# Trading the order of the two matmul widths between neighbouring output chunks of a decoder trunk on one core

## The chip, the cores and the metric

The kernel runs on one core of one Trainium2 chip. The metric is the device time of one execution in microseconds; less is better. Three executions of the kernel before took 2847.95, 2847.97 and 2849.41 us, median 2847.97.

## What is computed

A decoder trunk of two layers over 256 tokens of width 2048, in float32, with 256 memory tokens to attend to. Nearly all of the work is matrix products with weights that are read once:

```python
for l in range(DEPTH):                       # DEPTH = 2, D_MODEL = 2048, D_FF = 8192
    hn = rms_norm(x, mix_norm_g[l])
    x = x + (even_mixer(hn, ...) if l % 2 == 0 else odd_mixer(hn, ...))
    x = x + cross_attention(rms_norm(x, xattn_norm_g[l]), mem_n, xq_w[l], xk_w[l], xv_w[l], xo_w[l])
    x = x + sq_relu_mlp(rms_norm(x, mlp_norm_g[l]), mlp_w1[l], mlp_w2[l])
return rms_norm(x, final_norm_g)
```

`even_mixer` is a gated convolution beside a differential attention, `odd_mixer` a gated short convolution; both end in a product with an output weight (`even_out`, `odd_out`).

## The kernel before

**The product.** Activations lie transposed: 128 partitions of a channel chunk, 256 tokens along the row. A weight column block of 128 outputs is an "output chunk" and needs 16 products over the 16 chunks of the input width (2048 = 16 x 128). To keep float32 accuracy every operand is split in two parts of a shorter format: `hi`, a rounded copy, and `lo`, the rest. TensorE computes hi x hi and hi x lo of the activations in one instruction, because the activation's two parts lie side by side (`act.both(k)`, 512 columns); the weight's rest needs a second one, lo x hi (`act.hi(k)`, 256 columns). So an output chunk is 16 products of 512 columns with weights `whi` and 16 of 256 columns with weights `wlo`, all summed in one PSUM bank; a 256-column product touches the first half of the bank only. Each product has a weight load of its own (PEld in the profile).

**The weights' way.** A chunk's weights come in two halves (g = 0 and 1) of 128 x 1024, enough for eight products each. SyncE's queue loads a half to a `raw` buffer (4 buffers), ScalarE casts it to `whi` (3 buffers, `wspl`), VectorE subtracts to get `wlo` (4 buffers). With three `whi` buffers and two halves a chunk, the first half of chunk c+1 goes where the second half of chunk c-1 was, and the second half of chunk c+1 goes where the first half of chunk c was. ScalarE and VectorE work through their instructions in order.

**Long runs.** `long_run` (L219) writes a chunk's 32 products: 15 of 512 columns (L229), 16 of 256 (L231), and the sixteenth of 512 as the last (L233). `proj_long` (L236) uses it in the mixers' and the cross-attention's output projections and in `odd_in`, `Chunk.run` (L968) in the MLP and at the end of `odd_mixer`.

**Pieces.** `proj_group` and `proj` (L206, L241) take the two halves one after the other, so that a chunk can begin when its first half is there. `wide_piece` (L193) writes a half: eight products of 512 and eight of 256; in the last half the eighth of 512 comes last. `cross` uses it for the 32 query chunks `xq` (16 a layer).

**The MLP.** `mlp` (L1139) goes through four quarters of 2048 hidden channels in each of the two layers. A quarter begins with 16 first-product chunks (`firsts`, L1235, c = 0 to 15), and here the order on every engine is that of the code. While TensorE runs chunk c, the other engines do this in order:

- ScalarE copies half of the PSUM bank of chunk c-1 (`sum`), casts the first half of chunk c+1 (`n.hi(0)`), casts its second half (`n.hi(1)`), and squares the output of chunk c-1 (`uu`).
- VectorE adds and scales the output of chunk c-1 (two instructions on `sum`), then makes `n.lo(0)` and `n.lo(1)` of chunk c+1.
- For c = 5, 9 and 13, behind that, VectorE does two additions on `uu` (L1278, L1279), ScalarE casts the result to `hs` (L1280) and VectorE subtracts (L1281).

The second half of a quarter (steps of a Strassen form, and chunks by `outs[k].run`) calls `long_run` too, without the change's new argument.

Of the kernel before, what the change touches and what calls it, by code (L numbers as in the profile page):

```python
# [10 lines left out]
F32 = mybir.dt.float32  # L11
# [6 lines left out]
P = 128  # L18
D = 2048
S = 256  # L20
# [25 lines left out]
def trunk(ctx: ExitStack, tc: tile.TileContext, d):  # L46
# [38 lines left out]
    ps_mm = ctx.enter_context(tc.tile_pool(name="ps_mm", bufs=4, space=bass.MemoryType.PSUM))  # L85
# [59 lines left out]
    def ordered(i, token):  # L145

        tc.stamp_issue_order_token(i.ins, token)
# [20 lines left out]
    def mm(*a, **k):  # L168
        i = T.matmul(*a, **k)  # L169
        if strict[0]:  # L170
            ordered(i, "pe")
# [18 lines left out]
            ordered(V.tensor_tensor(lo[:, o], raw[:, o], f(hi[:, o]), op=ALU.subtract), "lo")  # L190
        return hi, lo

    def wide_piece(ps, hi, lo, act, k, first, last, between=None):  # L193


        w = [slice(j * P, (j + 1) * P) for j in range(8)]
        for j in range(7 if last else 8):
            mm(ps, hi[:, w[j]], act.both(k + j), start=first and j == 0, stop=False)
        for j in range(8):
            mm(ps[:, :S], lo[:, w[j]], act.hi(k + j), start=False, stop=False)  # L200
        if between:
            between()
        if last:
            mm(ps, hi[:, w[7]], act.both(k + 7), start=False, stop=True)

    def proj_group(srcs, act, order=(0, 1), between=None):  # L206


        pp = [ps_mm.tile([P, 512], F32, tag="mm", name="mm") for _ in srcs]
        for g in order:  # L210
            if g == order[-1] and len(srcs) > 1:
                run_stages(END)
            for src, ps in zip(srcs, pp):
                hi, lo = weights(src[:, g * 1024:(g + 1) * 1024])
                first, last = g == order[0], g == order[-1]
                wide_piece(ps, hi, lo, act, g * 8, first, last, between if last and ps is pp[-1] else None)
        return pp

    def long_run(ps, h, l, act, narrow=False):  # L219

        w = [slice(j * P, (j + 1) * P) for j in range(8)]
        if narrow:
            for k in range(16):
                for part in (act.lo, act.hi):
                    mm(ps[:, :S], h[k // 8][:, w[k % 8]], part(k), start=k == 0 and part == act.lo, stop=False)
            for k in range(16):
                mm(ps[:, :S], l[k // 8][:, w[k % 8]], act.hi(k), start=False, stop=k == 15)
            return ps
        for k in range(15):  # L229
            mm(ps, h[k // 8][:, w[k % 8]], act.both(k), start=k == 0, stop=False)  # L230
        for k in range(16):  # L231
            mm(ps[:, :S], l[k // 8][:, w[k % 8]], act.hi(k), start=False, stop=False)
        mm(ps, h[1][:, w[7]], act.both(15), start=False, stop=True)  # L233
        return ps

    def proj_long(src, act):  # L236
        ps = ps_mm.tile([P, 512], F32, tag="mm", name="mm")
        h, l = zip(*[weights(src[:, g * 1024:(g + 1) * 1024]) for g in range(2)])
        return long_run(ps, h, l, act)

    def proj(src, act):  # L241
        return proj_group([src], act)[0]

    def summed(ps, out=None):

        t = tmp32("sum")
        A.copy(t, ps[:, S:])
        out = t if out is None else out
        V.tensor_tensor(out, ps[:, :S], t, op=ALU.add)
        return out  # L250
# [46 lines left out]
    def joined(*acts):  # L297
        a = Act(0, "")
        a.t = [t for b in acts for t in b.t]
        return a  # L300
# [112 lines left out]
    def even_mixer():  # L413
        xa, ss = Act(NC, "xn"), SumSq()
        w = d["even_in"]
# [224 lines left out]
        cat_a, cat_o = ln["cat"], rr["co"]  # L640
        nxt, nss = Act(NC, "xn"), SumSq()
        cat = joined(cat_a, cat_o)
        for c, ps in enumerate(proj_group([d["even_out"][c] for c in range(3)], cat, (1, 0))):
            residual(c, ps, nxt, nss, "xat0")
        for c in range(3, NC):
# [4 lines left out]
    def odd_mixer(xa, ss):  # L650
        w = d["odd_in"]
        y, m = Act(NC, "y"), Act(NC, "mem")
        begun = [NC, 2 * NC, 0, NC + 1]
        rows = []

        def mean():
# [14 lines left out]
        for c in range(NC):  # L671
# [7 lines left out]
            i = c * 3  # L679
            V.tensor_scalar(uu, cc, col("conv_c_w", i + 2), None, op0=ALU.mult)  # L680
            for j in range(2):
                s = 2 - j
# [26 lines left out]
            V.tensor_tensor(t[:, :, 1], q, f(t[:, :, 0]), op=ALU.subtract)  # L709

        LAST = 4
        for c in range(NC - LAST):
            residual(c, proj_long(d["odd_out"][c], y), None, nss, "xat1")
            if c < 8:
                forms(c)
# [47 lines left out]
        for k in range(NC):  # L763
            last = k + 1 == NC
# [20 lines left out]
            s = st[k + 1]  # L785
# [70 lines left out]
    def cross(l, xa, ss, kmem):  # L856
        keys, vals = kmem
        r = None
        scale = 512 ** -0.5
        oa = joined()  # L860

        def scores(h, q, k):
            v = split(vals[h // 2][:, h % 2], [2, 512])
            pr = []
            for t in range(2):
                tq = slice(t * P, (t + 1) * P)
                ps = ps_at.tile([P, 512], F32, tag="at", name="sx")[:, :S]
                for i in range(4):
                    mm(ps, q[:, 0, i, tq], k[:, 0, i], start=i == 0, stop=False)
                    mm(ps, q[:, 1, i, tq], k[:, 0, i], start=False, stop=False)  # L870
                    mm(ps, q[:, 0, i, tq], k[:, 1, i], start=False, stop=i == 3)
                p, inv = softmax_rows(ps, mem_r["bc"], S, scale)
                V.tensor_scalar(p, p, inv, None, op0=ALU.mult)
                pr.append(p)
            stage(X1, lambda: turn(h, pr, v))

        def turn(h, pr, v):
            pt = ps_at.tile([P, 512], F32, tag="at", name="ptx")
            for t in range(2):
                for kt in range(2):  # L880
                    transpose(out=pt[:, kt * S + t * P:kt * S + (t + 1) * P], in_=pr[t][:, kt * P:(kt + 1) * P],
                              identity=ident)
            pb = pools["att"].tile([P, 2, 512], F32R, tag="pt", name="pb")
            A.copy(pb[:, 0], pt)
            V.tensor_tensor(pb[:, 1], pt, f(pb[:, 0]), op=ALU.subtract)
            stage(X2, lambda: heads_out(h, pb, v))

        def heads_out(h, pb, v):
            if h % 2 == 0:
                oa.t += Act(8, "o").t  # L890
            for i in range(4):
                if i % 2 == 0:
                    bank = ps_at.tile([P, 512], F32, tag="at", name="pox")
                po = bank[:, i % 2 * S:(i % 2 + 1) * S]
                e = slice(i * P, (i + 1) * P)
                for kt in range(2):
                    c = slice(kt * S, (kt + 1) * S)
                    mm(po, v[:, 0, kt, e], pb[:, 0, c], start=kt == 0, stop=False)
                    mm(po, v[:, 1, kt, e], pb[:, 0, c], start=False, stop=False)
                    mm(po, v[:, 0, kt, e], pb[:, 1, c], start=False, stop=kt == 1)  # L900
                if i % 2:
                    oa.put2(4 * h + i - 1, bank)

        for h in range(XH):
            q = half.tile([P, 2, 4, S], F32R, tag="half", name="xq")
            for i in range(4):
                if i == 3:
                    k = split(keys[h // 2][:, h % 2], [4, S])
                s = summed(proj(d[f"xq{l}"][4 * h + i], xa))
                if r is None:  # L910
                    r = rstd(ss.acc, D)
                    strict[0] = True
                V.tensor_tensor(s, s, r, op=ALU.mult)
                A.copy(q[:, 0, i], s)
                V.tensor_tensor(q[:, 1, i], s, f(q[:, 0, i]), op=ALU.subtract)
            stage(X0, lambda h=h, q=q, k=k: scores(h, q, k))
        nxt, nss = Act(NC, "xn"), SumSq()

        for c, ps in enumerate(proj_group([d[f"xo{l}"][c] for c in range(4)], oa)):
            residual(c, ps, nxt, nss, f"mlp{l}")  # L920
        strict[0] = False
        for c in range(4, NC):
            residual(c, proj_long(d[f"xo{l}"][c], oa), nxt, nss, f"mlp{l}")
        return nxt, nss
# [15 lines left out]
    class Chunk:  # L940
# [24 lines left out]
            A.activation(self.l[g], self.raw[g], AF.Copy, scale=-1.0)  # L965
            G.dma_start(out=self.l[g], in_=self.raw[g], accum_op=ALU.add)  # L966

        def run(self, act, pool, tag, narrow=False):  # L968
            self.ps = long_run(pool.tile([P, 512], F32, tag=tag, name="mm"), self.h, self.l, act, narrow)

    class Step:

# [166 lines left out]
    def mlp(l, xa, ss, gname):  # L1139
# [13 lines left out]
        turn = [0]  # L1153
# [69 lines left out]
        for qd in range(4):  # L1223
            seven, closing = qd < ns, qd == 3
            hid, sa, vs = Act(0, "hid"), [], {}
            chunks, outs = firsts[qd], seconds[qd]
# [6 lines left out]
                return vs[c // 4]  # L1233

            for c in range(NC):  # L1235
                chunks[c].run(xa, ps_mm, "mm")
                fetch((Chunk, Step))
                if c in (4, 13) and seven:
                    st[c // 13].load()
# [30 lines left out]
                g = c // 4 - 1  # L1270
# [11 lines left out]
                if seven:  # L1282
                    s = st[0]
# [12 lines left out]
            if seven:  # L1296
# [6 lines left out]
                for k in range(8):  # L1303
                    st[k].run(sevens.pp, hid, sa, k)
                    fetch(Step)
                    w = outs[k]
# [17 lines left out]
                    if k < 7:  # L1324
                        s = st[k + 1]
# [168 lines left out]
```

## Time and profile before

| what | value |
|---|---|
| three executions | 2847.95 to 2849.41 us, median 2847.97 |
| the profiled execution | 2848.45 us, span of its instructions 2846.1 us |
| PE busy | 2834.7 us of the span, 15843 products |
| VectorE (DVE) busy | 2318.1 us, 81% |
| ScalarE (ACT) busy | 1689.5 us, 59% |
| granted TensorE clock | 0.999 |
| DMA | 588 MB, 207 GB/s |

PE is TensorE's products, PEld its weight loads. In a timeline a row's first number is the start in us from the span's start, the second the time to the end of the last of its instructions, and in square brackets stands how long the engine was idle before it and what ended that. A product's own duration in the profile overlaps the next one; what a product costs is the distance from its start to the next one's start. So a row's cost is read from the start of the next row.

### The profile page before, as it was taken

Reading aid. Unit: us, or ns where it says so; the run is one execution under the profiler, and the core shown is the slowest. Engines: PE = TensorE matmul, PEld = TensorE weight load, DVE = VectorE, ACT = ScalarE, POOL = GpSimd, SP = SyncE. Lnnn points to the kernel's source line nnn. Section 1 sums busy time; section 2 is a strip of 40 time slices with the busy share of each in tenths; the row PEclk is TensorE's granted clock in tenths of the full one; section 3 lists DMA queues with packets and bytes.
Section 4 is the critical chain, followed back from the end, with each engine's and each line's share of the span. In section 5 each row is a group of like instructions: output and inputs, shape, how many; then the busy total and the mean of one; then the engine's idle time right before and its main releaser. Section 6 shows DMA issues by size and latency. Waiting matters only on the chain.

```text
span 2846.1 us, 42267 instructions
## 1 busy us (share of the span) xinstructions
PE 2834.7 (100%) x15843; PEld 2478.3 (87%) x15843; DVE 2318.1 (81%) x3602; ACT 1689.5 (59%) x2368; POOL 78.6 (3%) x107
## 2 busy tenths in 40 slices
PE   9999999999999999999999999999999999999998
PEld 8888888898888888888888888888988888888887
DVE  7899987777788888888987787888777888888888
ACT  6665445555565665656654455676556656656566
POOL 0000000000000000000000000000000000000000
PEclk9999999999999999999999999999999999999999
DMA  7455665545686786967765566994456867769676
GB/s 249 160 189 172 192 194 189 171 149 178 195 256 195 223 241 200 266 193 234 214 203 199 196 209 224 253 255 155 150 178 194 253 209 218 234 200 262 199 236 179
DMA packets 213516, 588.23 MB, mean 207 GB/s; under 512 B 18240, under 2 KB 84160, under 8 KB 213312
## 3 DMA queue, kind: packets, MB, share of 16 engines
q1 hardware_dynamic: 200064, 538.54, 58.1%
q0 software_dynamic: 12672, 46.14, 8.2%
q8 instruction: 124, 2.03, 0.3%
q10 hardware_dynamic: 576, 0.85, 0.1%
q14 instruction: 80, 0.66, 0.1%
HBM read 537.23 MB, written 2.10 MB: 189 GB/s over the span
## 4 chain that ended last, share of the span: by engine, by line
PE 97%; DMA 1%; DVE 1%; ACT 1%; issue 0%; SPq 0%; DVEq 0%; POOLq 0%; POOL 0%; ACTq 0%
PE mm L169 77%; PE p L169 13%; PE mmr L169 4%; PE pox L169 1%; PE sx L169 1%; DMA wlo<-raw 0%; PE sc L169 0%; DVE x L59 0%; DMA raw<-w 0%; ACT whi L59 0%; PE nmr L169 0%; PE po L169 0%; DVE wlo L59 0%; DMA raw<-odd_in 0%; DMA x<-xT 0%
## 5 line engine op out<-in xcount | busy, mean ns | idle before, releaser
L59 ACT CAST whi<-raw 128x1024 fp32r<-128x1024 f32 (+1 forms) x849 | 890.6, 1050 | 394.2 <-PE mm L169 297.2
L59 DVE TENSOR_TENSOR wlo<-raw,whi 128x1024 fp32r<-128x1024 f32 (+1 forms) x761 | 924.0, 1220 | 93.2 <-ACT whi L59 82.6
L169 PE MATMUL mm<-xn,whi 128*128 128x512 f32 x3840 | 938.7, 392 | 0.0
L169 PEld LDWEIGHTS mm<-xn,whi 128*128 128x128 f32 x3840 | 702.0, 188 | 133.3 <-DVE xn L59 0.6
L169 PEld LDWEIGHTS mm<-xn,wlo 128*128 128x128 f32 x3840 | 501.1, 191 | 24.0
L169 PE MATMUL mm<-xn,wlo 128*128 128x256 f32 x3840 | 509.1, 283 | 0.0
L59 ACT COPY sum<-mm 128x256 f32<-128x256 f32 x272 | 100.6, 371 | 394.5 <-PE mm L169 394.0
L169 PE MATMUL mm<-hid,whi 128*128 128x512 f32 (+1 forms) x1040 | 253.4, 386 | 0.0
L59 ACT CAST tw<-raws 128x1024 fp32r<-128x1024 f32 x160 | 160.6, 1046 | 145.1 <-DVE raws L59 141.2
L59 DVE TENSOR_TENSOR raws<-raws 128x512 f32<-128x512 f32 x320 | 220.8, 690 | 7.6
L169 PEld LDWEIGHTS mm<-hid,whi 128*128 128x128 f32 x1040 | 193.5, 188 | 36.8
L59 DVE TENSOR_TENSOR sum<-mm,sum 128x256 f32<-128x256 f32 x240 | 100.9, 421 | 146.5 <-ACT sum L59 146.2
L59 DVE TENSOR_TENSOR tw<-raws,tw 128x1024 fp32r<-128x1024 f32 x160 | 189.6, 1222 | 26.2 <-ACT tw L59 24.6
L169 PE MATMUL p<-tw,hs 128*128 128x512 f32 x720 | 189.2, 389 | 0.0
L59 DVE TENSOR_TENSOR x<-x,mm 128x256 f32<-128x256 f32 x255 | 106.9, 420 | 81.7 <-PE mm L169 77.2
L169 PEld LDWEIGHTS p<-tw,hs 128*128 128x128 f32 x720 | 135.2, 188 | 28.0
L966 POOL DMA_DIRECT2D wlo<-raw x88 | 74.9, 855 | 2550.8 <-ACT wlo L59 1847.1
L169 PEld LDWEIGHTS mm<-hid,wlo 128*128 128x128 f32 x1024 | 131.1, 191 | 5.8 <-DMA wlo<-raw 1.1
L169 PE MATMUL mm<-hid,wlo 128*128 128x256 f32 x1024 | 133.1, 283 | 0.4 <-DMA wlo<-raw 0.4
L169 PE MATMUL mm<-mem,whi 128*128 128x512 f32 x512 | 128.5, 393 | 0.0
L169 PE MATMUL mm<-o,whi 128*128 128x512 f32 x512 | 124.7, 392 | 0.0
L59 DVE TENSOR_TENSOR slo<-raws,shi 128x1024 fp32r<-128x1024 f32 x71 | 86.9, 1224 | 38.1 <-ACT shi L59 38.1
(227 smaller groups left out, 3236.6 us busy)
## 6 DMA issues: line engine op xcount, KB each, us to landing
raw<-w SPq DMA_DIRECT2D x384, 512.0 KB, 5.0
raws<-w SPq DMA_DIRECT2D x128, 512.0 KB, 5.2
raw<-odd_in SPq DMA_DIRECT2D x96, 512.0 KB, 4.6
wlo<-raw POOLq DMA_DIRECT2D x88, 512.0 KB, 7.5
raw<-even_in SPq DMA_DIRECT2D x64, 512.0 KB, 4.4
raw<-xk SPq DMA_DIRECT2D x64, 512.0 KB, 4.6
raw<-xq SPq DMA_DIRECT2D x64, 512.0 KB, 4.2
raw<-xo SPq DMA_DIRECT2D x64, 512.0 KB, 3.8
```

What stands on the lines that cost most here:

```text
L59: i = getattr(self.engine, name)(*a, **k)
L169: i = T.matmul(*a, **k)
L966: G.dma_start(out=self.l[g], in_=self.raw[g], accum_op=ALU.add)
```

## The change

`long_run` gets an argument `turn`. With `turn=None` it is as before (15, 16, 1). With `turn=0` all 16 products of 512 columns come first and the 16 of 256 behind them; with `turn=1` one product of 512 comes first, then all 16 of 256, then the other 15 of 512. (The first must be of 512, since it opens the whole bank.) `proj_long` takes the two in turns, starting anew with 0 in each section; the MLP's first products take `c % 2`. Below, a chunk with `turn=0` is called even, one with `turn=1` odd. There are 110 odd ones: 6 in `even_out`, 22 in `odd_in`, 6 in `odd_out`, 6 in `xo` of each layer, and 8 in each of the MLP's eight quarters. The second halves of the query chunks (`fold`) begin with the 256-column products and end with the 512-column ones.

```diff
+        if fold and last:
+            for j in range(8):
+                mm(ps[:, :S], lo[:, w[j]], act.hi(k + j), start=False, stop=False)
+            for j in range(8):
+                mm(ps, hi[:, w[j]], act.both(k + j), start=False, stop=j == 7)
+            return
...
-        for k in range(15):
+        split = 15 if turn is None else 1 if turn else 16
+        for k in range(split):
             mm(ps, h[k // 8][:, w[k % 8]], act.both(k), start=k == 0, stop=False)
         for k in range(16):
-            mm(ps[:, :S], l[k // 8][:, w[k % 8]], act.hi(k), start=False, stop=False)
-        mm(ps, h[1][:, w[7]], act.both(15), start=False, stop=True)
+            mm(ps[:, :S], l[k // 8][:, w[k % 8]], act.hi(k), start=False, stop=split == 16 and k == 15)
+        for k in range(split, 16):
+            mm(ps, h[k // 8][:, w[k % 8]], act.both(k), start=False, stop=k == 15)
         return ps
...
-        return long_run(ps, h, l, act)
+        longs[0] ^= 1
+        return long_run(ps, h, l, act, turn=1 - longs[0])
...
-                s = summed(proj(d[f"xq{l}"][4 * h + i], xa))
+                s = summed(proj(d[f"xq{l}"][4 * h + i], xa, True))
...
-                chunks[c].run(xa, ps_mm, "mm")
+                chunks[c].run(xa, ps_mm, "mm", turn=c % 2)
```

The first place is TensorE in the MLP's second quarter of the first layer, chunk c = 9 of the first products, an odd one. `whi_9745` and `whi_9749` are the two halves' hi parts, `wlo_9751` and `wlo_9753` their lo parts, `xn` the activations. Before:

```order
L169 MATMUL mm_9761<-xn_6711,whi_9745 128x512 x4
L169 MATMUL mm_9761<-xn_6712,whi_9745 128x512 x4
L169 MATMUL mm_9761<-xn_6713,whi_9749 128x512 x4
L169 MATMUL mm_9761<-xn_6714,whi_9749 128x512 x3
L169 MATMUL mm_9761<-xn_6711,wlo_9751 128x256 x4
L169 MATMUL mm_9761<-xn_6712,wlo_9751 128x256 x4
L169 MATMUL mm_9761<-xn_6713,wlo_9753 128x256 x4
L169 MATMUL mm_9761<-xn_6714,wlo_9753 128x256 x4
L169 MATMUL mm_9761<-xn_6714,whi_9749 128x512
```

The same chunk on TensorE now:

```order
L169 MATMUL mm_9761<-xn_6711,whi_9745 128x512
L169 MATMUL mm_9761<-xn_6711,wlo_9751 128x256 x4
L169 MATMUL mm_9761<-xn_6712,wlo_9751 128x256 x4
L169 MATMUL mm_9761<-xn_6713,wlo_9753 128x256 x4
L169 MATMUL mm_9761<-xn_6714,wlo_9753 128x256 x4
L169 MATMUL mm_9761<-xn_6711,whi_9745 128x512 x3
L169 MATMUL mm_9761<-xn_6712,whi_9745 128x512 x4
L169 MATMUL mm_9761<-xn_6713,whi_9749 128x512 x4
L169 MATMUL mm_9761<-xn_6714,whi_9749 128x512 x4
```

Both lo parts are read 14 products earlier in the chunk than before, and the last read of the first half's hi part (`whi_9745`) comes behind all 16 of the 256-column products.

The second place is VectorE at the same time: what it does while TensorE runs chunks 9 and 10. `wlo_9807` and `wlo_9809` belong to chunk 10, `hs` is the combined hidden piece, `mm_9761` the output of chunk 9, `wlo_9862` and `wlo_9864` belong to chunk 11. These rows are the same in both kernels:

```order
L59 TENSOR_TENSOR wlo_9807<-raw_9739,whi_9801 128x1024
L59 TENSOR_TENSOR wlo_9809<-raw_9740,whi_9805 128x1024
L59 TENSOR_TENSOR uu_9578<-uu_9578 128x2x128 x2
L59 TENSOR_TENSOR hs_9814<-uu_9578,hs_9814 128x8x128
L59 TENSOR_TENSOR sum_9854<-mm_9761,sum_9854 128x256
L59 SCALAR_TENSOR_TENSOR sum_9854<-sum_9854,rb_7766 128x256
L59 TENSOR_TENSOR wlo_9862<-raw_9794,whi_9856 128x1024
L59 TENSOR_TENSOR wlo_9864<-raw_9795,whi_9860 128x1024
```

Nothing moved here; the instructions around `wlo_9809`, which needs `whi_9805`, keep their order in both kernels, and `whi_9805` is written to the buffer that `whi_9745` leaves.

The third place is TensorE in the first cross-attention, at query chunks behind the first head's output (`pox`). Before:

```order
L169 MATMUL mm<-xn,whi 128x512 x8
L169 MATMUL mm<-xn,wlo 128x256 x8
L169 MATMUL mm<-xn,whi 128x512 x7
L169 MATMUL mm<-xn,wlo 128x256 x8
L169 MATMUL mm<-xn,whi 128x512 x9
L169 MATMUL mm<-xn,wlo 128x256 x8
```

The same stretch on TensorE now:

```order
L169 MATMUL mm<-xn,whi 128x512 x8
L169 MATMUL mm<-xn,wlo 128x256 x16
L169 MATMUL mm<-xn,whi 128x512 x16
L169 MATMUL mm<-xn,wlo 128x256 x16
L169 MATMUL mm<-xn,whi 128x512 x16
```

The eight 256-column products of a chunk's second half come seven products earlier, right behind those of the first half.

More of the change, by code (lines that the diff above doesn't have):

```diff
@@ L191, in weights, with wide_piece @@
         return hi, lo
-    def wide_piece(ps, hi, lo, act, k, first, last, between=None):
+    def wide_piece(ps, hi, lo, act, k, first, last, between=None, fold=False):
         w = [slice(j * P, (j + 1) * P) for j in range(8)]
+        if fold and last:
[4 more added lines that the diff above has]
+            return
         for j in range(7 if last else 8):
@@ L204, in wide_piece, with proj_group @@
             mm(ps, hi[:, w[7]], act.both(k + 7), start=False, stop=True)
-    def proj_group(srcs, act, order=(0, 1), between=None):
+    def proj_group(srcs, act, order=(0, 1), between=None, fold=False):
         pp = [ps_mm.tile([P, 512], F32, tag="mm", name="mm") for _ in srcs]
@@ L215, in proj_group, with long_run @@
                 first, last = g == order[0], g == order[-1]
-                wide_piece(ps, hi, lo, act, g * 8, first, last, between if last and ps is pp[-1] else None)
+                wide_piece(ps, hi, lo, act, g * 8, first, last, between if last and ps is pp[-1] else None, fold)
         return pp
-    def long_run(ps, h, l, act, narrow=False):
+    def long_run(ps, h, l, act, narrow=False, turn=None):
         w = [slice(j * P, (j + 1) * P) for j in range(8)]
@@ L228, in long_run @@
             return ps
-        for k in range(15):
+        split = 15 if turn is None else 1 if turn else 16
+        for k in range(split):
             mm(ps, h[k // 8][:, w[k % 8]], act.both(k), start=k == 0, stop=False)
         for k in range(16):
-            mm(ps[:, :S], l[k // 8][:, w[k % 8]], act.hi(k), start=False, stop=False)
-        mm(ps, h[1][:, w[7]], act.both(15), start=False, stop=True)
+            mm(ps[:, :S], l[k // 8][:, w[k % 8]], act.hi(k), start=False, stop=split == 16 and k == 15)
+        for k in range(split, 16):
+            mm(ps, h[k // 8][:, w[k % 8]], act.both(k), start=False, stop=k == 15)
         return ps
+    longs = [0]
     def proj_long(src, act):
@@ L238, in proj_long, with proj @@
         h, l = zip(*[weights(src[:, g * 1024:(g + 1) * 1024]) for g in range(2)])
-        return long_run(ps, h, l, act)
-    def proj(src, act):
-        return proj_group([src], act)[0]
+        longs[0] ^= 1
+        return long_run(ps, h, l, act, turn=1 - longs[0])
+    def proj(src, act, fold=False):
+        return proj_group([src], act, fold=fold)[0]
     def summed(ps, out=None):
@@ L642, in even_mixer @@
         cat = joined(cat_a, cat_o)
+        longs[0] = 0
         for c, ps in enumerate(proj_group([d["even_out"][c] for c in range(3)], cat, (1, 0))):
@@ L653, in odd_mixer @@
         begun = [NC, 2 * NC, 0, NC + 1]
+        longs[0] = 0
         rows = []
@@ L711, in odd_mixer @@
         LAST = 4
+        longs[0] = 0
         for c in range(NC - LAST):
@@ L917, in cross @@
         nxt, nss = Act(NC, "xn"), SumSq()
+        longs[0] = 0
         for c, ps in enumerate(proj_group([d[f"xo{l}"][c] for c in range(4)], oa)):
@@ L966, in lo_added, with run @@
             G.dma_start(out=self.l[g], in_=self.raw[g], accum_op=ALU.add)
-        def run(self, act, pool, tag, narrow=False):
-            self.ps = long_run(pool.tile([P, 512], F32, tag=tag, name="mm"), self.h, self.l, act, narrow)
+        def run(self, act, pool, tag, narrow=False, turn=None):
+            self.ps = long_run(pool.tile([P, 512], F32, tag=tag, name="mm"), self.h, self.l, act, narrow, turn)
     class Step:
```

## Prediction

> **What bounds the kernel now.** I read the page first: the busy times and the chain that ended last.
>
> ```profile
> PE 2834.7 (100%) x15843; PEld 2478.3 (87%) x15843; DVE 2318.1 (81%) x3602; ACT 1689.5 (59%) x2368; POOL 78.6 (3%) x107
> PE 97%; DMA 1%; DVE 1%; ACT 1%; issue 0%; SPq 0%; DVEq 0%; POOLq 0%; POOL 0%; ACTq 0%
> ```
>
> TensorE works all the time, and 97% of the chain is its own. So two things can change the time: the distance from product to product, and new waits of TensorE. VectorE is 81% busy on average; where it is busier than that is where a wait can come from. For the distances I took the timeline of TensorE in a stretch of long runs (cross-attention's output projection), then one where 512-column products follow others of 512.
>
> ```profile
> 706.50 2.08 PE L169 MATMUL mm<-o,wlo 128*128 128x256 f32 x16
> 708.41 3.82 PE L169 MATMUL mm<-o,whi 128*128 128x512 f32 x16
> 712.07 2.08 PE L169 MATMUL mm<-o,wlo 128*128 128x256 f32 x16
> 713.98 3.82 PE L169 MATMUL mm<-o,whi 128*128 128x512 f32 x16
> ```
>
> ```profile
> 1003.77 3.56 PE L169 MATMUL mm<-hid,whi 128*128 128x512 f32 x15
> 1007.17 2.08 PE L169 MATMUL mm<-hid,wlo 128*128 128x256 f32 x16
> ```
>
> ```profile
> 558.30 0.40 PE L169 MATMUL mm<-xn,whi 128*128 128x512 f32 x1
> 558.54 3.05 PE L169 MATMUL pox<-pb,hl 128*128 128x256 f32 x24
> 561.42 1.99 PE L169 MATMUL mm<-xn,whi 128*128 128x512 f32 x8
> ```
>
> From start to start, 15 products of 512 behind others of 512 take 1007.17 - 1003.77 = 3.40 us, 0.227 each. 24 products of 256 take 561.42 - 558.54 = 2.88, 0.120 each. A whole cycle of 16 and 16 takes 713.98 - 708.41 = 5.57, where 16 x 0.227 + 16 x 0.120 = 5.55: going over to the other width and back costs 0.02 us. The lone product of 512 between two runs of 256 (558.30) takes 0.24, about 0.013 over its 0.227.
>
> **The change part by part: the switches.** Before, two neighbouring long chunks go through two cycles, 2 x 0.02 of switches. Now the run of 512 is once 31 long and once a lone one: 0.02 + 0.013. That saves 0.007 us for each of the 110 odd chunks, 0.8 us; if the lone one is free it is 0.02 each, 2.2 us. A query chunk went to 256 and back twice and now does so once: 0.02 x 32 = 0.6 us. I take 1.5 us saved in all, between 1.4 and 2.8. No product is added or removed.
>
> A rule of the Trainium skill ("TensorE: Matmul & The Clock Gate", section "Back-to-back issue gap") gives a single product's gap at full clock as its columns at 2.4 GHz plus 2.5 ns, so 0.109 and 0.216 us, with no term for what went before; by it the switches would be free and nothing saved. The rows above differ from it in all three (0.120, 0.227 and the 0.02), so I go by the rows.
>
> **The lo parts come earlier in odd chunks.** The first 256-column product of a chunk now stands 14 products of 512 nearer to its start: 14 x 0.227 and the switch, 3.20 us. The 16 of 256 need two lo parts in about 2 us. Who has that much to spare? The tightest place is the MLP, where VectorE does most beside the lo parts. All engines' timeline in the second quarter of the first MLP, TensorE at chunk 9, others preparing 10 and 11:
>
> ```profile
> 949.46 3.82 PE L169 MATMUL mm<-xn,whi 128*128 128x512 f32 x16
> ...
> 951.51 2.54 DVE L59 TENSOR_TENSOR wlo<-raw,whi 128x1024 fp32r<-128x1024 f32 x2
> 951.73 1.06 ACT L59 CAST whi<-raw 128x1024 fp32r<-128x1024 f32 x1 [0.51 <-PE mm L169]
> ...
> 953.12 2.08 PE L169 MATMUL mm<-xn,wlo 128*128 128x256 f32 x16
> 953.96 0.88 DVE L59 TENSOR_TENSOR uu<-uu 128x256 f32<-128x256 f32 x2
> 954.87 1.05 ACT L59 CAST hs<-uu 128x1024 fp32r<-128x1024 f32 x1 [1.77 <-DVE uu L59]
> ...
> 955.03 3.82 PE L169 MATMUL mm<-xn,whi 128*128 128x512 f32 x16
> ...
> 955.96 1.23 DVE L59 TENSOR_TENSOR hs<-uu,hs 128x1024 fp32r<-128x1024 f32 x1 [1.12 <-ACT hs L59]
> ...
> 957.10 0.42 DVE L59 TENSOR_TENSOR sum<-mm,sum 128x256 f32<-128x256 f32 x1
> ...
> 957.55 0.43 DVE L59 SCALAR_TENSOR_TENSOR sum<-sum,rb 128x256 f32<-128x256 f32 x1
> 957.89 2.36 DVE L59 TENSOR_TENSOR wlo<-raw,whi 128x1024 fp32r<-128x1024 f32 x2
> ...
> 958.68 2.08 PE L169 MATMUL mm<-xn,wlo 128*128 128x256 f32 x16
> ```
>
> One row has the length of a lo part, from the groups by form:
>
> ```profile
> L59 DVE TENSOR_TENSOR wlo<-raw,whi 128x1024 fp32r<-128x1024 f32 x759 | 922.7, 1222 | 93.1 <-ACT whi L59 82.6
> ```
>
> Read it as a chain. The cast at 951.73 (chunk 10's second half) waited for TensorE: its buffer is that of chunk 9's first half. From it on, each row follows the one before without a gap: chunk 10's second lo part, two additions, the cast to hs, the subtraction (955.96), two instructions on chunk 9's sum, chunk 11's lo parts. The first of these is ready at 957.89 + 1.22 = 959.11, the second at 957.89 + 2.36 = 960.25, 1.14 later. Chunk 11 first reads them a chunk after 958.68, at 958.68 + 5.57 = 964.25: now 5.14 us to spare.
>
> The change takes from that twice. Chunk 11 is odd: its use comes 3.20 earlier. Chunk 9 is odd too: its eighth 512-column product, which frees the buffer, goes behind the 16 of 256, so that the cast at 951.73 starts 955.03 - 953.12 = 1.91 later, and with the switch 1.92; and the whole chain behind it, in which VectorE and ScalarE wait only for each other, moves along. Left are 5.14 - 3.20 - 1.92 = 0.02 us. That is too little, because a part that is ready is not at once a product:
>
> ```profile
> 647.89 0.69 DVE L59 TENSOR_TENSOR o<-pox,o 128x512 fp32r<-128x512 f32 x1 [0.75 <-ACT o L59]
> 648.64 0.19 PEld L169 LDWEIGHTS mm<-o,whi 128*128 128x128 f32 x1 [0.45 <-DVE o L59]
> ...
> 648.98 0.40 PE L169 MATMUL mm<-o,wlo 128*128 128x256 f32 x2
> ```
>
> VectorE ends at 648.58, the weight load starts 0.06 later, and the next product but one follows 0.34 behind the load where one distance is 0.227: 0.11 of it is the load with nothing to cover it. So 0.17 us from ready to product, and TensorE loses 0.17 - 0.02 = 0.15 at the first lo part. The second comes 1.14 behind the first, and the eight products on the first last 8 x 0.120 = 0.96: another 0.18. Together 0.33 us.
>
> How often? Only where hs is made beside first products of an odd chunk, c = 5, 9 and 13, with the loss at 7, 11 and 15. The group has
>
> ```profile
> L59 DVE TENSOR_TENSOR hs<-uu,hs 128x1024 fp32r<-128x1024 f32 x32 | 39.2, 1224 | 26.8 <-ACT hs L59 26.8
> ```
>
> 32 rows, four a quarter, one of them in the quarter's second half: 3 x 8 = 24 times. 24 x 0.33 = 7.9 us. The bounds: 0 if the chain is 0.33 shorter than I make it, and 24 x 0.53 = 12.7 if it is 0.2 longer.
>
> **Elsewhere the cover should hold.** In the output projection the second lo part is the later one:
>
> ```profile
> 706.27 1.22 DVE L59 TENSOR_TENSOR wlo<-raw,whi 128x1024 fp32r<-128x1024 f32 x1
> ```
>
> It is ready at 707.49 and used behind the first eight of the run that begins at 712.07, at 713.03: 5.54 to spare. Its cast follows an even chunk, whose buffers are freed as before, so only the 3.20 goes: 2.3 left. Even chunks get their second cast 1.92 later but use it where they did: 3.6 left. For the query chunks' second half, from the timelines of VectorE and TensorE:
>
> ```profile
> 565.03 1.22 DVE L59 TENSOR_TENSOR wlo<-raw,whi 128x1024 fp32r<-128x1024 f32 x1
> ```
>
> ```profile
> 569.79 1.78 PE L169 MATMUL mm<-xn,whi 128*128 128x512 f32 x7
> 571.41 1.12 PE L169 MATMUL mm<-xn,wlo 128*128 128x256 f32 x8
> ```
>
> Ready at 566.25, used at 571.41, now at 569.79: 3.5 left. I put these at nothing; each 0.1 us missed in each of the 46 odd chunks outside the MLP would cost 4.6.
>
> **The sum.** The profiled execution's 2848.45 us + 7.9 - 1.5 = 2854.85, and it lies 0.48 over the median of the runs. So 2854.4 is forecast, 6.4 us (0.22%) over the median. About 0.2%, 5.7 us, is what a measurement of this kernel can tell from no change, so this is hardly outside: the stall has to be 0.30 a time at least.
>
> **The rivals.**
>
> - *The cover holds in the MLP* (not slower). The place is the first 256-column product of chunks 7, 11 and 15; it decides whether the first lo part is there 0.17 us before its turn. For it: by my sum 0.02 is left, and 0.33 less of chain, in a chain of ten links over 9 us, would do it. Against it: its links are fixed durations, and the cast's start hangs on one product of TensorE. Then the switches' saving stands alone: 2848.0 - 1.5 = 2846.5. Chance 0.19.
> - *Waits in the other sections too.* There the order of VectorE's instructions is a scheduler's, and a burst (the convolution's multiplications, the softmax) can stand ahead of a lo part that is now due earlier. For it: the odd chunks there have half the room. Against it: 2.3 and 3.5 us. With 0.15 us in each of the 46: 2854.4 + 6.9 = 2861.3. Chance 0.12.
> - *The switches were never a cost*, and what I read from the rows is in the record alone: then nothing is saved, 2854.4 + 1.5 = 2855.9. It is what the gap formula of the Trainium skill, in the section named above, would make of it. Against it: whole cycles, not single products, show the 0.02. Chance 0.04.
> - *Faster by over 0.2%.* All that the rows allow is 2.8 us; more would need a switch that costs twice what they show. Chance 0.03.
>
> **How the numbers follow.** My forecast has 0.62, with 0.2 to 0.5 us a stall: 2851.3 to 2858.5 of its own. Within it, stalls over 0.30 have two thirds (0.41), under it a third (0.21). Slower: 0.41 + 0.12 + 0.04 = 0.57. Within 0.2%: 0.21 + 0.19 = 0.40. Faster: 0.03. The range goes from most of the cover's case to just short of the waits in other sections: 2847.0 to 2860.5.
>
> **What would show it.** Right: in the MLP's first products, in chunks 7, 11 and 15, weight loads of wlo with an idle time put down to VectorE's wlo, two a chunk, 0.1 to 0.25 us each, 48 in all; the cast of an even chunk's second half about 3.95 us behind the start of the odd one, where it was 2.0; a query chunk 0.02 shorter. Wrong: no such waits, or waits of weight loads in the output projections or the gated convolution's chunks; a pair of long chunks that isn't between 11.11 and 11.14 us where nothing waits.

## The result and the profile after

| | before | after |
|---|---|---|
| median of five executions | 2847.97 us | 2869.18 us |
| lowest to highest | 2847.95 to 2849.41 | 2866.64 to 2870.51 |
| profiled execution, span | 2848.45, 2846.1 | 2867.46, 2865.7 |
| granted clock | 0.999 | 0.999 |

The ratio of the mean times is 1.0072, 95% interval 1.0061 to 1.0083. By the medians the kernel is slower by 21.2 us, where 6.4 were forecast, and outside the range. The span of the profiled execution is 19.6 us longer than that of before, and nearly all of this can be followed in the traces. The chain that ended last, by engine, on the page of after:

```profile
PE 93%; DMA 5%; issue 1%; DVE 1%; ACT 0%; SPq 0%; POOLq 0%; POOL 0%; DVEq 0%
```

TensorE had 97% of it and DMA 1%; now DMA has 5%. The waits of TensorE's weight loads in after (total us, times, longest) say which DMA:

```profile
PEld mm L169 <- DMA wlo<-raw: 12.1, 8, 1.9
PEld mm L169 <- DVE wlo L59: 5.3, 26, 0.5
```

The second row is the wait that was forecast. The first was not: eight waits, one a quarter, for `wlo<-raw`, a lo part that comes by DMA. These are the products concerned, in the second half of each MLP quarter, in the groups of before and then of after:

```profile
L169 PEld LDWEIGHTS mm<-hid,wlo 128*128 128x128 f32 x1024 | 131.1, 191 | 5.8 <-DMA wlo<-raw 1.1
L169 PE MATMUL mm<-hid,wlo 128*128 128x256 f32 x1024 | 133.1, 283 | 0.4 <-DMA wlo<-raw 0.4
```

```profile
L169 PEld LDWEIGHTS mm<-hid,wlo 128*128 128x128 f32 x1024 | 130.6, 191 | 16.4 <-DMA wlo<-raw 12.1
L169 PE MATMUL mm<-hid,wlo 128*128 128x256 f32 x1024 | 133.7, 284 | 8.8 <-DMA wlo<-raw 8.8
```

The page of before had the hint: 0.4 us, a wait of the products in one quarter out of eight, where there should be none if there were room.

**The forecast place.** TensorE in after, second quarter; chunk 9 (odd) starts at 952.74, chunk 11 at 963.89:

```profile
954.89 7.25 PE L169 MATMUL mm<-xn,whi 128*128 128x512 f32 x31
961.98 2.08 PE L169 MATMUL mm<-xn,wlo 128*128 128x256 f32 x16
963.89 0.39 PE L169 MATMUL mm<-xn,whi 128*128 128x512 f32 x1
964.16 2.36 PE L169 MATMUL mm<-xn,wlo 128*128 128x256 f32 x16
966.35 7.22 PE L169 MATMUL mm<-xn,whi 128*128 128x512 f32 x31
```

ScalarE's cast of chunk 10's second half, and VectorE behind it:

```profile
956.73 1.05 ACT L59 CAST whi<-raw 128x1024 fp32r<-128x1024 f32 x1 [2.46 <-PE mm L169]
```

```profile
957.81 1.23 DVE L59 TENSOR_TENSOR wlo<-raw,whi 128x1024 fp32r<-128x1024 f32 x1 [0.94 <-ACT whi L59]
...
960.95 1.23 DVE L59 TENSOR_TENSOR hs<-uu,hs 128x1024 fp32r<-128x1024 f32 x1 [1.12 <-ACT hs L59]
...
962.89 2.35 DVE L59 TENSOR_TENSOR wlo<-raw,whi 128x1024 fp32r<-128x1024 f32 x2
```

The cast is 956.73 - 952.74 = 3.99 us behind the chunk's start, and chunk 11's lo parts follow at 962.89. Chunk 9 is an odd chunk too, but waits for nothing. Against it, chunk 11's lone 512-column product takes 0.27 in place of 0.23, and its 16 products of 256 take 966.35 - 964.16 = 2.19 in place of 1.92. The second lo part is first used by the ninth of them, here in a view that starts with it:

```profile
965.30 1.22 PE L169 MATMUL mm<-xn,wlo 128*128 128x256 f32 x8
```

So the first eight take 1.14 and the other eight 1.05, where 0.96 is usual. By the trace's single products, averaged over all such chunks, the first lo part costs 0.14 us (0.03 of it on the lone product) and the second 0.18; the products behind them then take 0.05 less. In all, an odd chunk that waits takes 0.27 us longer than one that doesn't.

**The other place.** Chunk 15 of the first quarter starts at 811.29 in before and 812.47 in after. Before, VectorE makes chunk 15's lo parts, SyncE's queue issues loads as buffers come free, GpSimd issues the two accumulating DMAs, and TensorE runs the first output chunk of the second half:

```profile
808.35 2.35 DVE L59 TENSOR_TENSOR wlo<-raw,whi 128x1024 fp32r<-128x1024 f32 x2
```

```profile
803.22 7.84 SPq L949 DMA_DIRECT2D raw<-w  x4
811.11 0.98 SPq L981 DMA_DIRECT2D raws<-w  x2
```

```profile
814.14 1.89 POOL L966 DMA_DIRECT2D wlo<-raw  x2 [615.48 <-ACT wlo L59]
```

```profile
821.64 3.56 PE L169 MATMUL mm<-hid,whi 128*128 128x512 f32 x15
825.06 2.18 PE L169 MATMUL mm<-hid,wlo 128*128 128x256 f32 x16
```

The same in after:

```profile
811.47 2.36 DVE L59 TENSOR_TENSOR wlo<-raw,whi 128x1024 fp32r<-128x1024 f32 x2
```

```profile
804.81 9.37 SPq L964 DMA_DIRECT2D raw<-w  x4
814.23 0.98 SPq L996 DMA_DIRECT2D raws<-w  x2
```

```profile
815.32 1.89 POOL L981 DMA_DIRECT2D wlo<-raw  x2 [616.04 <-PE mm L169]
```

```profile
823.13 3.56 PE L169 MATMUL mm<-hid,whi 128*128 128x512 f32 x15
827.77 2.17 PE L169 MATMUL mm<-hid,wlo 128*128 128x256 f32 x16 [1.08 <-DMA wlo<-raw]
```

Count from chunk 15's start. The accumulating DMAs are issued 2.85 us behind it in both kernels. The lo parts were begun 2.94 ahead of it and are now begun 1.00 ahead: 1.94 later. They release the `raw` buffers, so the last of the four `raw` loads and the two `raws` loads behind it (512 KB each) move along: `raws` from 0.18 ahead of the chunk's start to 1.76 behind it. They now stand directly in front of the accumulating DMAs. What the queues moved between 816 and 820 us, before and then after (packets, MB, share of 16 engines):

```profile
q0 software_dynamic: 151, 0.57, 71.6%
q1 hardware_dynamic: 478, 0.47, 34.4%
```

```profile
q1 hardware_dynamic: 650, 0.98, 87.2%
```

GpSimd's queue is q0, SyncE's q1; the window begins 1.9 us behind the first issue in before and 0.7 behind it in after. In after not one packet of q0 moved in these four microseconds. By the trace's packet records the first one came 2.5 us behind the issue in before and 4.9 us behind it in after. It is the same in the other seven quarters: 1.9 to 2.6 us in before, 3.6 to 5.3 in after. TensorE needs the parts 3.4 us behind its first product of the output chunk, and waits.

Laid side by side, product by product, the two traces account for 19.4 of the 19.6 us by which the span grew:

- 6.4 us: 24 waits for lo parts at chunks 7, 11 and 15, 0.25 to 0.28 each.
- 10.1 us: eight DMA stalls, 0.45 to 1.79 each (against before, where one quarter had such a stall already).
- 2.2 us: a pair of an even and an odd chunk takes 11.15 us without its waits, 0.02 longer than two chunks of before, 110 times.
- 0.7 us: once, at the first odd chunk of `odd_in`.
- -0.6 us: the query chunks.
- 0.6 us: the first 30 us, where no instruction changed and where the runs below differ from before by -0.1 to 0.8.

### The profile page after: what moved, and what is told of

It reads as the page before. It is cut to its first block, busy times and chain, and to the rows that moved or that the text cites. A ratio compares the mean times of both kernels' runs of the same rounds, so it can differ in the third digit from the quotient of the medians.

```text
span 2865.7 us, 42247 instructions
## 1 busy us (share of the span) xinstructions
PE 2844.4 (99%) x15843; PEld 2478.1 (86%) x15843; DVE 2312.1 (81%) x3602; ACT 1692.4 (59%) x2368; POOL 78.6 (3%) x107
## 4 chain that ended last, share of the span: by engine, by line
PE 93%; DMA 5%; issue 1%; DVE 1%; ACT 0%; SPq 0%; POOLq 0%; POOL 0%; DVEq 0%
PE mm L169 74%; PE p L169 12%; PE mmr L169 4%; DMA wlo<-raw 3%; DMA raw<-w 1%; PE sx L169 1%; PE pox L169 1%; DVE wlo L59 0%; ACT whi L59 0%; PE sc L169 0%; PE nmr L169 0%; PE po L169 0%; DMA x<-xT 0%; DVE sum L59 0%; PE xt L174 0%
## 5 line engine op out<-in xcount | busy, mean ns | idle before, releaser
L169 PEld LDWEIGHTS mm<-hid,wlo 128*128 128x128 f32 x1024 | 130.6, 191 | 16.4 <-DMA wlo<-raw 12.1
```

## The experiments

Every time stands beside runs of the kernel before on the same chip: 2848.51 us for the first four runs, 2848.08 for the next four, 2848.29 for the last three. Stalls are differences between the traces, found as above: lo-part stalls against an odd chunk that waits for nothing, DMA stalls against before. An "odd" chunk has the order 1, 16, 15, a "plain" one that of before; where nothing else is said, the rest of the change stays in.

| run | odd chunks in the MLP | median us | ratio to before, 95% | lo-part stalls | DMA stalls |
|---|---|---|---|---|---|
| after | 1, 3, ... 15 | 2869.18 | 1.0061 to 1.0083 | 24, 6.4 us | 10.1 us |
| e1 | none | 2849.26 | 0.9994 to 1.0012 | none | none |
| e2 | 1, 3, ... 11, 15 | 2856.23 | 1.0017 to 1.0037 | 16, 4.3 us | 2.1 us |
| e3 | 1, 3, ... 13 | 2872.08 | 1.0067 to 1.0094 | 16, 4.2 us | 17.9 us |
| e8 | other order, see below | 2850.44 | 0.9995 to 1.0013 | none | 0.4 us |
| e9 | other order, see below | 2861.87 | 1.0035 to 1.0062 | none | 13.6 us |
| e5 | other order, see below | 2847.95 | 0.9991 to 1.0008 | none | under 0.2 us |
| e4 | as after | 2856.72 | 1.0018 to 1.0041 | 24 | none |
| e11 | as after | 2856.25 | 1.0018 to 1.0039 | 24 | none |
| e7 | 2, 4, ... 12 | 2860.94 | 1.0032 to 1.0057 | none | 11.8 us |
| e10 | 2, 4, ... 10 | 2848.05 | 0.9991 to 1.0009 | none | 0.4 us |
| e6 | none; only the fold | 2847.87 | 0.9990 to 1.0007 | none | as before |

**Is it all in the MLP?** Run e1:

```diff
-                chunks[c].run(xa, ps_mm, "mm", turn=c % 2)
+                chunks[c].run(xa, ps_mm, "mm")
```

> The MLP's first products go back to the order of before (15 of 512, 16 of 256, one of 512); the alternation in the other sections and the folded query chunks stay. The trace of after shows 24 stalls of 0.31 to 0.37 us at MLP chunks 7, 11 and 15, and eight of 0.4 to 1.8 us at the first 256-column products of each quarter's second half. Theory L (late loads: everything comes from the MLP's odd chunks): both go, the fold still saves 0.6 us and the other sections lose about 1 us, so 2848.5 us, within 0.1% of before. Rival O (the odd chunks of the other sections cost something too): only what lies in the MLP goes, and 5 us or more over before stay, 2853 or more.

2849.26 us, 0.75 over before; the span is 1.2 us longer. Rival O is out: fold and other sections together cost about a microsecond.

**Which chunk makes the DMA late, 13 or 15?** Runs e2 and e3:

```diff
-                chunks[c].run(xa, ps_mm, "mm", turn=c % 2)
+                chunks[c].run(xa, ps_mm, "mm", turn=None if c == 13 else c % 2)
```

```diff
-                chunks[c].run(xa, ps_mm, "mm", turn=c % 2)
+                chunks[c].run(xa, ps_mm, "mm", turn=None if c == 15 else c % 2)
```

> As after, but chunk 13 of each MLP quarter has the order of before; chunk 15 stays odd. Theory L: what delays chunk 15's lo parts, and with them the loads that compete with the accumulating DMA, is that odd chunk 13 frees the buffer of its first half 1.92 us later. With 13 plain the chain is on time, chunk 15 has 5.14 - 3.20 = 1.9 us to spare, its eight stalls of 0.33 go, and the DMA stalls (about 10 us) go too: 16 x 0.33 = 5.3 and about 1 elsewhere are left, 2854 us. Rival F (chunk 15 being odd itself puts the accumulating DMA late): the DMA stalls stay, 2864 us.

> As after, but chunk 15 of each MLP quarter has the order of before; chunk 13 stays odd. Theory L: chunk 15's own stall (8 x 0.33 = 2.6 us) goes, but the chain and the loads are as late as in after, so the wait for the accumulating DMA takes back what chunk 15 no longer loses: no change against after, 2867 to 2869 us, with some 12 us of DMA stalls. Rival F: without an odd chunk 15 the DMA stalls go: 16 x 0.33 = 5.3 and 1 elsewhere, 2854 us.

With 13 plain, some 13 us are gone; with 15 plain, nothing is. So the order of chunk 15 is not the cause; what chunk 13 passes on is. In e2 `raws` was issued 0.07 us behind chunk 15's start (before: 0.18 ahead) and small DMA stalls are left in four quarters, so e2 ended 2 us over its figure: there is hardly a quarter of a microsecond of room. In e3 the DMA stalls grew from 10.1 to 17.9, by more than the 2.6 expected, and the time is 3 us over its figure. A halved clock in two quarters, told in the last section, makes 3.3 us of it; the rest, 2 us of longer waits, no run explains.

**Is it the buffer that comes free late, or the lo parts' earlier use?** Three orders of an odd chunk. In e8 the products of 512 come first, the second half's ahead of the first half's:

```diff
+        if turn == 2:
+            for k in (8, 9, 10, 11, 12, 13, 14, 15, 0, 1, 2, 3, 4, 5, 6, 7):
+                mm(ps, h[k // 8][:, w[k % 8]], act.both(k), start=k == 8, stop=False)
+            for k in range(16):
+                mm(ps[:, :S], l[k // 8][:, w[k % 8]], act.hi(k), start=False, stop=k == 15)
+            return ps
```

> The odd MLP chunks keep the lo parts where they were used (all 16 512-column products first), but take the second half's eight products ahead of the first half's, so that the first half's buffer comes free 8 x 0.227 = 1.8 us later, about as late as in after. No lo part is used earlier than in before. Theory L: no stall at chunks 7, 11 and 15 (5.14 - 1.8 = 3.3 us to spare), but the loads are late and the DMA stalls come, 8 to 12 us in all: 2857 us (2855 to 2860). Rival F (the earlier use is what it takes): 2848 us.

The time can't be told from that of before, but e8 did not do what it was made for. ScalarE's cast behind the start of chunk 13 (799.92) in e8:

```profile
801.96 1.06 ACT L59 CAST whi<-raw 128x1024 fp32r<-128x1024 f32 x1 [0.52 <-PE mm L169]
```

It comes 2.04 us behind the start, as in before: it takes whichever of the two buffers is free first, and that is now the second half's. Nothing was late, so e8 tells nothing between the theories. In e9 both halves are in use until the 15th product:

```diff
-            for k in (8, 9, 10, 11, 12, 13, 14, 15, 0, 1, 2, 3, 4, 5, 6, 7):
+            for k in (0, 1, 2, 3, 4, 5, 6, 8, 9, 10, 11, 12, 13, 14, 7, 15):
```

> The kernel with the two halves' products in swapped order (16 of 512 first) did not free a buffer later: its second half's buffer was then free first, and the cast went there, 1.81 us behind the chunk's start as in before. Here an odd MLP chunk runs its 16 products of 512 as seven of the first half, seven of the second, the eighth of the first, the eighth of the second, then 16 of 256: no buffer is free before the 15th product, 7 x 0.227 = 1.6 us later than in before, and no lo part is used earlier. Theory L: no stalls at chunks 7, 11 and 15, but the chain and the loads are 1.6 us late at chunk 15: DMA stalls of 0.5 to 1.3 us in most quarters, 4 to 10 us in all, 2853 to 2859 us. Rival F (it takes the earlier use): 2849 us.

The cast, chunk 13 starting at 799.96, and TensorE at the first 256-column products of the quarter's second half in e9:

```profile
803.58 1.05 ACT L59 CAST whi<-raw 128x1024 fp32r<-128x1024 f32 x1 [2.09 <-PE mm L169]
```

```profile
821.44 3.56 PE L169 MATMUL mm<-hid,whi 128*128 128x512 f32 x15
826.91 3.38 PE L169 MATMUL mm<-hid,wlo 128*128 128x256 f32 x16 [1.91 <-DMA wlo<-raw]
```

3.62 behind the start, 1.6 later; no stall at chunks 7, 11 and 15, and a DMA stall in every quarter, though no lo part is used any earlier. The late buffer alone makes them. The time is 3 us over the upper end of what was expected; half of that is the slowed clock of the last section. e5 is the opposite:

```diff
-        split = 15 if turn is None else 1 if turn else 16
+        split = 15 if turn is None else 8 if turn else 16
```

> As after, but an odd chunk runs 8 of 512, 16 of 256, 8 of 512: its lo parts are used 8 x 0.227 - 0.23 = 1.6 us later than in after (1.6 us earlier than in before), and its first half is done before the 256-column products, so that its buffer comes free when it did in before. Theory L: 5.14 - 1.6 = 3.5 us to spare at chunks 7, 11 and 15, no stalls there, the chain on time, no DMA stalls: 2849 us, as before within 0.1%. Rival F (using the lo parts earlier costs by itself): 8 us or more over before.

2847.95 us: lo parts used 1.6 us earlier with the buffer freed on time cost nothing. With e9, rival F is out.

**Do the accumulating DMAs wait for the loads?** e4 halves what is accumulated there, e11 moves only loads.

```diff
                 if c == NC - 1 and seven:
                     n.lo_added(1)
-                    n.lo_added(0)
+                    n.lo(0)
```

> As after, but at MLP chunk 15 the first lo part of the quarter's second half is made by VectorE (one subtraction of 1.22 us, 88 of the accumulating DMAs less eight); the second one stays an accumulating DMA. Theory L (TensorE waits there for the accumulating DMAs and for nothing else): half of their bytes go, the second part is due 0.96 us later, and the DMA stalls of the eight quarters (10 to 11 us) go or shrink to under 0.3 each; the 24 stalls of 0.32 stay: 2858 to 2860 us. Rival B (the DMA is only the last of several things that are late there by the same 2 us): something else is waited for, and 2865 us or more stay.

```diff
                 loads[-7].pop(0)
+                loads[-6].pop(0)
...
+                if c == NC - 1 and seven:
+                    st[2].load()
                 fetch((Chunk, Step))
```

> The kernel after, with one thing moved on SyncE's queue alone: the two loads of the third step (512 KB each), which stand right behind the two raw loads of the second output chunk and are issued some 1.1 us ahead of the first accumulating DMA of that place, go ahead of these raw loads, where their buffers are free 3 us earlier. No other engine's order changes; the accumulating DMAs are issued when they were. Theory L (the accumulating DMAs wait for the loads issued just ahead of them): half of these bytes are out of the way, the DMA stalls (11 us) go or shrink to under 0.4 each, and the 24 stalls of 0.31 stay: 2857 to 2861 us. Rival P (the accumulating DMAs are late by themselves, whatever is loaded beside them): 2868 us as after.

Both give back the 10 us of DMA stalls and keep the 24 others, some 1 us under what was expected. So rival B, that something else is late there too, is out. In e4 the one accumulating DMA that is left still moves its first packet 5.45 us behind its issue in the first quarter; TensorE doesn't wait: this part is the second one, needed 0.96 us later, and only half the bytes come that way. e11 is the cleaner one. Its SyncE queue, GpSimd, what the queues moved between 816 and 820 us, and the group of weight loads that had 12.1 us of waits:

```profile
808.25 3.13 SPq L996 DMA_DIRECT2D raws<-w  x2
812.93 11.95 SPq L964 DMA_DIRECT2D raw<-w  x4
```

```profile
815.54 1.89 POOL L981 DMA_DIRECT2D wlo<-raw  x2 [616.06 <-PE mm L169]
```

```profile
q0 software_dynamic: 131, 0.51, 64.1%
q1 hardware_dynamic: 190, 0.65, 40.9%
```

```profile
L169 PEld LDWEIGHTS mm<-hid,wlo 128*128 128x128 f32 x1024 | 131.2, 191 | 4.9
```

Chunk 15 starts at 812.69 here, so the accumulating DMAs are issued 2.85 behind it as ever; with `raws` out of the way, their first packet comes 1.6 us later (1.4 to 1.8 over the eight quarters), and TensorE waits for no DMA any more. Rival P is out.

**Does the place of the odd chunks decide?** In e7 the odd chunks are those that no extra chain precedes:

```diff
-                chunks[c].run(xa, ps_mm, "mm", turn=c % 2)
+                chunks[c].run(xa, ps_mm, "mm", turn=1 if c in (2, 4, 6, 8, 10, 12) else None)
```

> In the MLP the odd chunks are 2, 4, 6, 8, 10 and 12 instead of 1, 3, ... 15; all others have the order of before. They use their lo parts 3.2 us earlier and free the first half's buffer 1.92 us later just as in after, but no extra chain stands ahead of a lo part that is due in an odd chunk, and chunks 13 to 15 are on time. Theory L: no stalls, 2849 to 2850 us. Rival E (each odd chunk of the MLP costs about 0.1 us by itself, wherever it stands): 48 odd chunks, 5 us or more over before.

No stall in any chunk, as expected, yet 12.9 us slower: my theory was too narrow. The cast of chunk 13's second half (chunk 12 starts at 794.75), and SyncE's queue (chunk 15 starts at 811.42), in e7:

```profile
798.70 1.05 ACT L59 CAST whi<-raw 128x1024 fp32r<-128x1024 f32 x1 [2.37 <-PE mm L169]
```

```profile
805.29 7.67 SPq L964 DMA_DIRECT2D raw<-w  x4
813.01 0.98 SPq L996 DMA_DIRECT2D raws<-w  x2
```

Chunk 12 already hands on a cast 3.95 us behind its start, and `raws` is issued 1.59 behind chunk 15's: the delay passes through three chunks. From the cast of `hid` in chunk 12 to chunk 15's lo parts, VectorE and ScalarE only wait for each other, so nothing there catches up. e10 leaves chunk 12 plain too:

```diff
-                chunks[c].run(xa, ps_mm, "mm", turn=c % 2)
+                chunks[c].run(xa, ps_mm, "mm", turn=1 if c in (2, 4, 6, 8, 10) else None)
```

> In the MLP the odd chunks are 2, 4, 6, 8 and 10 alone. The run with 2 to 12 had no stall in a chunk, as expected, but eight DMA stalls of 1.1 to 1.8 us: its loads were 1.76 us late at chunk 15, though chunks 13 to 15 had the order of before. Theory L, mended: ScalarE and VectorE have no idle time from the extra chain's beginning at chunk 12 to chunk 15, so that what odd chunk 12 makes late stays late; without it the loads at chunk 15 come when they did in before and nothing stalls: 2848 to 2850 us. If the DMA stalls come from odd chunks as such, 40 of the 48 are left, and so are most of the 12 us: 2857 or more.

2848.05 us: 40 odd chunks, with lo parts used as early as in after, cost nothing where the delay has time to run out. Rival E, a price for every odd chunk, is out with it. These 40 even gained a little. Between two runs of 256 there are two products of 512 here, the plain chunk's last and the odd one's first, and the long run has 30. Second quarter, e10:

```profile
934.93 6.99 PE L169 MATMUL mm<-xn,whi 128*128 128x512 f32 x30
...
946.03 6.99 PE L169 MATMUL mm<-xn,whi 128*128 128x512 f32 x30
```

A pair takes 946.03 - 934.93 = 11.10 here (11.107 by single products in both e7 and e10), against 11.133 in before: 0.026 saved, where after's pairs lose 0.02.

**What do the switches save?** e6 keeps only the fold:

> Only the folded query chunks, no alternation anywhere. The trace of after shows query chunks 0.02 us shorter: 32 x 0.02 = 0.6 us less than before, 2847.4 us, under what the times can tell; in the trace, the query sections are 0.6 us shorter and nothing else moves. If the switches were never a cost: no section changes by over 0.2 us.

The times cannot tell it from before. In the trace, the query section of the first layer is 0.40 us shorter and that of the second 0.20, together the 0.6 that was forecast for the fold. The only other shifts, 0.6 in the first 30 us and 0.4 at the end of the first MLP, lie where no instruction changed.

## Why the prediction was wrong

**What bounds the kernel, and the 24 stalls: right.** They came at chunks 7, 11 and 15 of every quarter and nowhere else in the MLP's first products; the cast stands at 3.99 us for 3.95. The first lo part costs 0.14 us where 0.15 was forecast, the second 0.18 as forecast. With 0.05 won back behind them that is 0.27 a time and 6.4 us in all, against 0.33 and 7.9. The list of waits counts one a chunk and not two, because the weight loads' second idle time, 0.12 us at 965.29, is too short for the list. The rival that the cover holds there is out.

**The step that failed: "elsewhere the cover should hold ... I put these at nothing".** That step looked only for lo parts needed by odd chunks in other sections. I had written that the whole chain behind the late cast "moves along", and followed it to the next product. But the chain also releases `raw` buffers, the loads that wait for these stand on SyncE's queue, and other loads stand behind them; at a quarter's end they meet the accumulating DMAs, which had no room at all. That term, 10 us, was missing, and no rival held it: the range's upper end came from lo parts in other sections. e9 makes this term alone, e11 takes it alone away, and e2, e3 and e10 put its origin in chunk 12 or 13. Of the 13 us that the span grew beyond the forecast, it is the largest part; 3.0 are the alternation, below.

**The switches: right for the fold, wrong for the alternation.** The fold saved its 0.6. The alternation of the long chunks saved no 0.8 but cost 2.2 us, 0.02 a pair, which puts the sum 3.0 us off. TensorE in `odd_in`, before and then after; the rows that start within a run are from views that start there:

```profile
1495.74 3.82 PE L169 MATMUL mm<-xn,whi 128*128 128x512 f32 x16
...
1496.90 2.66 PE L169 MATMUL mm<-xn,whi 128*128 128x512 f32 x11
1499.39 2.08 PE L169 MATMUL mm<-xn,wlo 128*128 128x256 f32 x16
...
1506.87 3.82 PE L169 MATMUL mm<-xn,whi 128*128 128x512 f32 x16
```

```profile
1512.35 0.40 PE L169 MATMUL mm<-xn,whi 128*128 128x512 f32 x1
...
1514.50 7.25 PE L169 MATMUL mm<-xn,whi 128*128 128x512 f32 x31
...
1516.83 4.92 PE L169 MATMUL mm<-xn,whi 128*128 128x512 f32 x21
1521.59 2.08 PE L169 MATMUL mm<-xn,wlo 128*128 128x256 f32 x16
1523.50 0.40 PE L169 MATMUL mm<-xn,whi 128*128 128x512 f32 x1
```

A pair took 11.13 us and takes 1523.50 - 1512.35 = 11.15, outside the 11.11 to 11.14 that the prediction named. The switch that I read from the rows is there: behind a run of 256, the first five products of 512 take 1496.90 - 1495.74 = 1.16, 0.232 each, and the other eleven 1499.39 - 1496.90 = 2.49, 0.226 each. So the rival that the switches were never a cost is out. The step that failed is that the run of 31 would begin like a run of 16. Its first ten products take 1516.83 - 1514.50 = 2.33, 0.233 each, and the other 21 take 1521.59 - 1516.83 = 4.76, 0.227 each: the one long switch costs 0.06, where two of 0.03 were before, and the lone product adds its part. With two products of 512 between the narrow runs (e7, e10) or eight (e5, and the fold's query chunks) the long run begins with 0.03 as in before. Why one product is too few is open.

**Waits in the other sections: nearly right.** They came in one place, the first odd chunk of `odd_in`, where a scheduler had put VectorE's work on `sum` ahead of a lo part (0.7 us, in e1 as well). The other 45 odd chunks outside the MLP had no wait for a lo part, so this rival's 6.9 us did not come.

## What to carry to other kernels

When a step is moved, follow not only who waits for its result, but which buffers it frees, what is loaded into them, and which transfers stand behind these loads; a delay passes along engines that only wait for each other until one of them has idle time of its own. A small wait in the profile of before, here 0.4 us in one quarter of eight, can mark a place without room: look at what the change moves toward it, however far away the edit is. If a version is to use data earlier, see that it frees its inputs no later: the order 8, 16, 8 (e5) used the lo parts earlier and cost nothing, though no version here beat the kernel before by what can be measured. And when a saving is read from one pattern of products, look for that very pattern in a trace: one wide product between two narrow runs behaved unlike two.

## What the runs showed of the hardware

**The accumulating DMA starts behind the loads issued before it.** In the first quarter the time from its issue to its first packet was 2.5 us in before, 4.9 in after and 1.6 in e11. Each time a quarter of what the loads issued ahead of it moved behind that issue was then still to come (0.26 of 1.05 MB, 0.37 of 1.60 and 0.21 of 0.83). The Trainium skill ("DMA: Bandwidth & Descriptors", section "Queues, rings and completion order") says that a DMA engine takes turns between the queues that have work, packet by packet; the four microseconds in after with 650 packets of SyncE's queue and none of GpSimd's do not look like turns. Whether GpSimd's packets were not there yet or not served, the traces don't tell.

**A gap of little over 2 us can halve the clock.** In one quarter of e9 and two of e3, TensorE lost more time than it waited. In e9, first quarter, the distance from the last product before the wait to the first behind it was 2.3 us, and then the windows (busy time of PE, PEld, DVE, ACT and POOL, granted clock, DMA share, GB/s) read:

```profile
824.00:826.00 2.00, 1.00 (x5) 0.50 (x3) 1.52 (x3) 1.71 (x2) 0.00 (x0) 1.00 1.05 217
826.00:828.00 2.00, 1.09 (x7) 1.09 (x8) 2.00 (x3) 1.23 (x2) 0.00 (x0) 0.86 0.73 138
828.00:830.00 2.00, 2.00 (x11) 2.00 (x11) 0.07 (x1) 0.00 (x0) 0.00 (x0) 0.50 0.88 259
830.00:832.00 2.00, 2.00 (x9) 1.67 (x8) 1.21 (x3) 1.05 (x1) 0.00 (x0) 0.79 0.99 375
```

The clock fell to half, and the 16 products of 256 that began at 826.91 took 3.18 us, against 2.01 behind after's waits. By the trace's clock records it stayed there for 3.41 us. The same happened twice in e3, behind distances of 2.40 us (first quarter) and 2.15 us (fourth). It does not come every time: distances of 2.82 and 2.61 us in e3 and 2.65 in e9 left the next 16 products at 2.02. None of after's stalls, at most 1.9 us, did it. So the length of the gap alone does not decide. The stretches at full clock that end or begin with such a fall may say what does: those of 522.239 us (e3) and 822.612 us (e3 and e9) are 153 and 241 times 3.4133 us, so the clock seems to be set on a fixed grid of 3.41 us, and where a gap falls on it may matter; no run tests this. The Trainium skill ("TensorE: Matmul & The Clock Gate", section "Why this matters for your kernels") warns of gaps over about 3 us; here 2.15 was enough once.
